# Decoder trunk: each quarter of the second norm transposed once, and the planner taken on through the first two up-projection pairs

## The chip, the cores and the metric

One core of a Trainium2 chip. The metric is the device time of one execution in microseconds (us); lower is better. The engines are TensorE (PE, matmuls and transposes), VectorE (DVE), ScalarE (ACT), GpSimd (POOL) and SyncE (SP, which here issues the transfers). Each runs its own queue in order and waits on semaphores for the others.

## What is computed

One layer of a decoder trunk on x of 1024 x 1024 (tokens x channels), in float32:

```python
h = rmsnorm(x, w_norm_mix)
...                       # h @ w_mix_in, split into three mixers:
...                       # a short gated convolution, a gated DeltaNet of 4 heads (chunked delta rule),
...                       # a stick-breaking attention of 4 heads
x = x + jnp.concatenate([y_sc, y_gdn, y_sb], axis=-1) @ w_mix_out[l]
h = rmsnorm(x, w_norm_ffn[l])
u = causal_dwconv(h @ w_ffn_up[l], w_ffn_conv[l])
gate, val = jnp.split(u, 2, axis=-1)
x = x + (jax.nn.silu(gate) * val) @ w_ffn_down[l]
return rmsnorm(x, w_norm_final)
```

## The kernel before

Tokens come in NB = 8 blocks of 128. Matmuls keep float32 accuracy by splitting each operand into a high and a low part (names ending in h and l) and adding three products, hh, hl and lh.

**The mixing part.** The input projection (`pd`, L314 to L318), the attention (`pz`, `pa`, `po`), and the delta rule, which for each block transposes what `ld` holds (`pv`, `pk`, `pq`), forms `pkq`, solves a triangular system (`py`, `pw`), steps the state (`p1` to `p4`), and ends in `pco` and `pyt`. The decays come as `m` (`m2` with the block's number) from a scratch in memory (`gscr`); the block's result `yg` is written back to `yscr`.

**The output projection.** `mo_mm(n)` computes block n of `pmo` on PE in eight steps (k) of six matmuls of 128x512, DVE adds it to x (`xr`), ACT squares and takes the root, DVE multiplies: h2 of the block, 128 tokens x 1024 channels. Its halves LO and HI, for token blocks 0 to 3 and 4 to 7, are the four quarters B11, B21, B12, B22 of a 2 x 2 partition.

**The up-projection** goes in 22 pairs of 128 gate and 128 value columns (`Pair`, L1524 holds its matmuls). Each pair uses seven products of quarters (m1 to m7, 12 matmuls each) instead of eight. Weights enter as quarters A11, A12, A22 and sums S1 to S4 (`up_sum`), split by `up_split`; activations as seven factors, B11, B21, B22 and the differences T1 to T4, each 4 x 128 x 512 as h and l. The steps e1 to e7 take a product out of PSUM into `ug` and `uv`; ca, cb, cc, cs, cg are the convolution and the gate.

**The factors before.** `mo_tr_p` (and `mo_tr` for block 7) transposes B11 and B21 of blocks 0 to 3. For blocks 4 to 7 POOL forms differences of h2 in token layout, in place; T1 and B22 are transposed (`phT`, `phB`) between steps of `pmo`, and T2, T3 and T4 by `mo_late` between the products of pairs 0 and 1. ACT copies the high part out of PSUM and DVE subtracts it for the low part. That makes 28 groups of four 128x128 transposes.

**What sets the order.** For the mixing part and the output projection a planner, `Flow`, sets the order of every engine: processes (`fl.spawn`) ask for engine time with an estimate and a class (lower first), take and give tokens of each buffer pool, and wait for events (`now`, `wait`). From the first pair on the code's order was written by hand for PE, and the framework ordered DVE, ACT, POOL and SP until pair 1's m7. From pair 2 on all orders are by hand.

## Time and profile before

| | us |
|---|---|
| median of 3 runs | 1229.4 (1226.56 to 1230.95) |
| profiled execution | 1229.95 |
| its span | 1228.2 |
| PE busy | 1194.0 (97%) |
| DVE busy | 942.5 (77%) |
| ACT busy | 634.7 (52%) |
| POOL busy | 404.7 (33%) |

The granted clock of PE was 0.996 of full over the span. The profile's page gives shares over all of the span; the views used further down cut it into stretches, list what PE waited for, and show single instructions with the idle time ahead of them and what ended it. The delta rule's blocks lie between about 342 and 490 us, `pmo1` to `pmo7` between 488 and 576, pairs 0 and 1 between 576 and 637.

### The profile page before, as it was taken

Reading aid. Unit: us, or ns where it says so; the run is one execution under the profiler, and the core shown is the slowest. Engines: PE = TensorE matmul, PEld = TensorE weight load, DVE = VectorE, ACT = ScalarE, POOL = GpSimd, SP = SyncE. Lnnn points to the kernel's source line nnn. Section 1 sums busy time; section 2 is a strip of 40 time slices with the busy share of each in tenths; the row PEclk is TensorE's granted clock in tenths of the full one; section 3 lists DMA queues with packets and bytes.
Section 4 is the critical chain, followed back from the end, with each engine's and each line's share of the span. In section 5 each row is a group of like instructions: output and inputs, shape, how many; then the busy total and the mean of one; then the engine's idle time right before and its main releaser. Section 6 shows DMA issues by size and latency. Waiting matters only on the chain.

```text
span 1228.2 us, 16683 instructions
## 1 busy us (share of the span) xinstructions
PE 1194.0 (97%) x6131; PEld 993.0 (81%) x6131; DVE 942.5 (77%) x1317; ACT 634.7 (52%) x1085; POOL 404.7 (33%) x322
## 2 busy tenths in 40 slices
PE   8999999999999999999899999999999999999997
PEld 6798887887878889777688888888888887888886
DVE  3776789977984769445778888888888878985774
ACT  6766576868334453323554443544545534454554
POOL 3445443434244542014424444345442322001200
PEclk9999999999999999999999999999999999999999
DMA  9111132432352663434122433233332279852314
GB/s 345 56 56 41 56 125 88 123 96 86 111 150 70 154 203 118 155 111 153 35 77 87 129 108 115 74 95 124 112 112 78 95 264 357 300 139 80 103 52 146
DMA packets 87089, 152.76 MB, mean 124 GB/s; under 512 B 6592, under 2 KB 42464, under 8 KB 86752
## 3 DMA queue, kind: packets, MB, share of 16 engines
q1 hardware_dynamic: 86864, 151.59, 38.2%
q8 instruction: 48, 0.79, 0.3%
q14 instruction: 33, 0.27, 0.1%
q10 hardware_dynamic: 144, 0.10, 0.1%
HBM read 110.50 MB, written 41.17 MB: 123 GB/s over the span
## 4 chain that ended last, share of the span: by engine, by line
PE 80%; DVE 6%; ACT 5%; DMA 4%; issue 3%; POOL 1%; SPq 0%; POOLq 0%; ACTq 0%; DVEq 0%
PE pu L1524 18%; PE pz L1524 9%; PE pdx L1693 8%; PE pdzP L1693 7%; PE pd L314 5%; PE pd L316 5%; PE pd L318 5%; PE py L1524 4%; PE pmo L1304 2%; PE pmo L1302 2%; PE pmo L1300 2%; DMA wd<-wdn_in 1%; PE po L687 1%; DMA m<-gscr 1%; PE pa L665 1%
## 5 line engine op out<-in xcount | busy, mean ns | idle before, releaser
L234 POOL TENSOR_TENSOR sg<-sg,om 128x511 f32<-128x511 f32 (+3 forms) x64 | 60.6, 957 | 116.5 <-DVE om L650 60.7
L237 DVE SCALAR_TENSOR_TENSOR ua<-uv,ck,ua 128x1023 f32<-128x1023 f32 (+1 forms) x44 | 76.1, 1730 | 7.3 <-ACT ua L231 7.2
L234 POOL TENSOR_TENSOR ws<-wu 128x512 f32<-128x512 f32 x43 | 66.5, 1567 | 46.1 <-DMA wu<-wup_in 41.8
L237 DVE SCALAR_TENSOR_TENSOR ua<-ug,ck,ua 128x1023 f32<-128x1023 f32 (+1 forms) x44 | 76.1, 1730 | 0.8
L231 ACT ACTIVATE ua<-ug,ck 128x1024 f32<-128x1024 f32 x22 | 25.4, 1154 | 90.5 <-DVE ug L234 90.5
L1618 ACT ACTIVATE ua<-ua 128x1024 f32<-128x1024 f32 x22 | 23.3, 1061 | 80.4 <-DVE ua L237 80.4
L234 POOL TENSOR_TENSOR x<-x,wfb 128x512 f32<-128x512 f32 x8 | 12.8, 1634 | 126.4 <-ACT y L1709 126.4
L234 POOL TENSOR_TENSOR A<-wu,A 128x512 fp32r<-128x512 f32 x13 | 18.0, 1386 | 99.7 <-ACT A L229 99.7
L234 DVE TENSOR_TENSOR S<-ws,S 128x512 fp32r<-128x512 f32 x53 | 40.6, 771 | 9.0 <-ACT S L229 8.0
L234 DVE TENSOR_TENSOR at<-pa,at 128x512 fp32r<-128x512 f32 (+3 forms) x48 | 26.1, 550 | 22.4 <-ACT at L229 22.2
L229 ACT ACTIVATE S<-ws 128x512 fp32r<-128x512 f32 x53 | 33.3, 630 | 16.8 <-DVE ws L234 7.8
L234 POOL TENSOR_TENSOR h<-h,h 128x512 f32<-128x512 f32 x12 | 15.9, 1324 | 78.3 <-DVE h L237 70.6
L1300 PE MATMUL pmo<-wo,yh 128*128 128x512 f32 x128 | 41.4, 404 | 0.0
L229 ACT ACTIVATE at<-pa 128x512 fp32r<-128x512 f32 (+3 forms) x48 | 23.4, 488 | 33.0 <-PE pa L665 31.7
L1302 PE MATMUL pmo<-wo,yh 128*128 128x512 f32 x128 | 39.7, 391 | 0.0
L1304 PE MATMUL pmo<-wo,yr 128*128 128x512 f32 x128 | 39.6, 390 | 0.0
L650 DVE TENSOR_TENSOR_SCAN om<-om 128x512 f32<-128x512 f32 (+3 forms) x32 | 33.7, 1067 | 6.9 <-ACT om L641 6.1
L1524 PE MATMUL pz<-fT1h,S 128*128 128x512 f32 x112 | 37.0, 391 | 1.6 <-DVE S L234 1.1
L234 DVE TENSOR_TENSOR ws<-ws,wu 128x512 f32<-128x512 f32 x22 | 27.0, 1226 | 14.7 <-POOL ws L234 14.7
L1524 PE MATMUL pu<-fT4h,A 128*128 128x512 f32 x104 | 35.4, 402 | 2.1 <-DVE uv L234 2.1
L229 ACT ACTIVATE ug<-pu 128x512 f32<-128x512 f32 x44 | 26.1, 594 | 15.8 <-PE pu L1524 15.7
L1524 PE MATMUL pz<-fB22h,S 128*128 128x512 f32 x104 | 34.1, 389 | 0.0
(1455 smaller groups left out, 4001.5 us busy)
## 6 DMA issues: line engine op xcount, KB each, us to landing
wu<-wup_in SPq DMA_DIRECT2D x44, 512.0 KB, 3.8
gaP<-gst SPq DMA_DIRECT2D x77, 256.0 KB, 3.4
w<-wcm_in SPq DMA_DIRECT2D x23, 512.0 KB, 3.6
wd<-wdn_in SPq DMA_DIRECT2D x44, 256.0 KB, 5.4
gst<-g SPq DMA_DIRECT2D x12, 512.0 KB, 2.7
...
```

The source lines that it names most:

```text
L229: nc.scalar.activation(out_, in_, AF.Copy)
L234: eng.tensor_tensor(out_, a, b, op=op)
L237: nc.vector.scalar_tensor_tensor(out_, a, s, b, op0=op0, op1=op1)
L314: nc.tensor.matmul(ps[th], lhsT=w_h, rhs=xh[k // 2][:, k % 2, th * 512:(th + 1) * 512], start=first, stop=False)
L316: nc.tensor.matmul(ps[th], lhsT=w_h, rhs=xl[k // 2][:, k % 2, th * 512:(th + 1) * 512], start=False, stop=False)
L318: nc.tensor.matmul(ps[th], lhsT=w_l, rhs=xh[k // 2][:, k % 2, th * 512:(th + 1) * 512], start=False, stop=last)
L650: nc.vector.tensor_tensor_scan(om[:, 0:w][:, ::-1], om[:, 0:w][:, ::-1], om[:, 0:w][:, ::-1], init, op0=mul, op1=ALU.bypass)
L1300: nc.tensor.matmul(po[:, c * 512:(c + 1) * 512], lhsT=h, rhs=wh_[:, c * 512:(c + 1) * 512], start=first, stop=False)
L1302: nc.tensor.matmul(po[:, c * 512:(c + 1) * 512], lhsT=h, rhs=wl_[:, c * 512:(c + 1) * 512], start=False, stop=False)
L1304: nc.tensor.matmul(po[:, c * 512:(c + 1) * 512], lhsT=l, rhs=wh_[:, c * 512:(c + 1) * 512], start=False, stop=last)
L1524: nc.tensor.matmul(o, lhsT=w[:, wk], rhs=b[:, k, :], start=first and k + j == 0, stop=k == 3 and j == 2, skip_group_check=not first)
L1693: nc.tensor.matmul(o, lhsT=a[:, tk], rhs=b, start=first and u == 0 and j == 0, stop=u == NU - 1 and j == 2, skip_group_check=not first)
```

## The change

Each quarter of h2 is transposed once. `left_half` does it for B11 and B21 and keeps a raw copy (`raw_b`) beside the split; `right_half` transposes the two quarters of blocks 4 to 7 (`ph12`, `ph22`) in one group of eight, forms t1 and T3 from them, and spawns the rest (`last_two`, `split_f`), so that all differences are made by DVE from transposed quarters. 64 transposes remain of 112. A group waits for the event "mid" of the next block, five steps into it.

The planner runs on to the end of pair 1: `products` asks for PE, `up_op` for the splits, `up_sums` for the sums (DVE, but POOL for pair 2's S1 and S3), `product_out` for e1 to e7, `first_gate` for pair 0's convolution. Pair 0's weights lie in buffers of the pool e8, which has 10 instead of 8, and the planner counts 8 tokens of it instead of 6; the delta rule's processes take tokens of the same pool.

```diff
+        elif r[0] == "sleep":
+            self.at(self.now + r[1], self.resume, proc, cls)
...
-        back, self.now = self.now, t + ns + land + T_AFTER[e]
+        back, self.now = self.now, t + ns + land + (0 if what == "more" else T_AFTER[e])
...
-    BIG = dict(x8=(8, 8192), e8=(8, 8192), at=(2, 4096), cv=(4, 4096), s2=(9, 2048), wr=(2, 4352), wh=(2, 4352), wl=(2, 4352), rb=(1, 4096))
+    BIG = dict(x8=(8, 8192), e8=(10, 8192), at=(2, 4096), cv=(4, 4096), s2=(9, 2048), wr=(2, 4352), wh=(2, 4352), wl=(2, 4352), rb=(1, 4096))
...
-    fl = Flow(mm=2, ms=4, cv=1, s2=9, wr=2, wh=2, wl=2, at=2, e8=6, x8=0)
...
+    fl = Flow(mm=2, ms=4, cv=1, s2=9, wr=2, wh=2, wl=2, at=2, e8=8, x8=0)
...
+        if n >= NB // 2:
+            fl.spawn(right_half(n), 2)
...
-            yield pe(T_STEP, 1000 + n)
+            yield pe(T_STEP, 1000 + n, "more")
...
+            if k == ks[KT // 2]:
+                now("mid", n)
+            if n == NB - 1:
+                fl.give("x8")
...
-        yield take(H2_TAG[n])
-        yield act(D)
-        h2 = cv(f"h2{n}", tag=H2_TAG[n])
+        yield take("at")
+        yield act(D, cls=1)
+        h2 = cv(f"h2{n}", tag="at")
...
+        for half in (LO, HI) if n < NB // 2 else ():
+            fl.spawn(left_half(n, half), 5)
...
+    def turned(ph, src):
         for k in range(4):
             nc.tensor.transpose(out=ph[:, k * P:(k + 1) * P], in_=src[:, k * P:(k + 1) * P], identity=ident)
-        t = slice(n * P, (n + 1) * P)
-        dh, dl = (f[:, :, t] for f in FAC[what])
-        phv = ph.rearrange("p (k t) -> p k t", k=4)
-        copy(dh, phv)
-        tt(nc.vector, dl, phv, f32(dh), sub)
...
-        m = n - NB // 2
-        h1 = mo[m]
-        tt(nc.gpsimd, h1[:, LO], h2[:, LO], h1[:, LO], sub)
-        factor("T1", m, h1[:, LO], e8)
-        factor("B22", m, h2[:, HI], e8)
-        tt(nc.gpsimd, h2[:, LO], h2[:, HI], h2[:, LO], sub)
-        tt(nc.gpsimd, h2[:, HI], h2[:, HI], h1[:, LO], sub)
-        tt(nc.gpsimd, h1[:, HI], h1[:, HI], h2[:, HI], sub)
...
+    def settled(n):
+
+        return wait("mid", n + 1) if n < NB - 1 else ("sleep", 500)
+
+    def left_half(m, half):
+
+        what, tag = ("B11", "wh") if half is LO else ("B21", "wr")
+        if m == 0:
...
+            make_factor(what, e8)
+        if m % 2 == 0:
+            yield take(tag)
+            pair = T([P, 2, HALF], F32, tag, f"r{what}{m}")
+            for a in range(2):
+                raw_b[what, m + a] = pair[:, a, :]
+        yield settled(m)
         yield take("ms")
         yield pe(4 * 109, 500)
...
+        ph = ms(f"ph{what}{m}")
+        turned(ph, mo[m][:, half])
+        now("turned", what, m)
+        dh, dl = tokens(what, m)
         yield act(512)
-        copy(dh, phv)
+        copy(raw_b[what, m], ph)
+        now("raw", what, m)
+        yield act(512)
+        copy(dh, kt(ph))
         yield dve(512, False)
-        tt(nc.vector, dl, phv, f32(dh), sub)
+        tt(nc.vector, dl, kt(ph), f32(dh), sub)
         fl.give("ms")
-
-    def mo_tr_p(n):
+        now("F", what, m)
...
+    def right_half(n):
+        m = n - NT
+        for what in ("B11", "B21"):
+            yield wait("raw", what, m)
+        b11, b21 = raw_b["B11", m], raw_b["B21", m]
+        if m == 0:
+            yield take("e8", 4)
+            for what in ("T1", "B22"):
+                make_factor(what, e8)
+        yield take("s2", 2)
+        now("right", n)
         yield wait("h2", n)
...
+        yield settled(n)
+        yield take("ms", 2)
+        yield pe(8 * 109, 500)
+        p12, p22 = ms(f"ph12{m}"), ms(f"ph22{m}")
+        turned(p12, mo[n][:, LO])
+        turned(p22, mo[n][:, HI])
+        fl.give("at")
+        t1, b22 = s2(f"t1{m}"), s2(f"b22{m}")
+        yield dve(512, False)
+        tt(nc.vector, t1, p12, b11, sub)
+        fl.spawn(split_f("T1", m, t1), 2)
+        yield act(512)
+        copy(b22, p22)
+        yield dve(512, False)
+        tt(nc.vector, b11, b22, p12, sub)
+        fl.spawn(split_f("T3", m, b11), 7)
+        fl.spawn(last_two(m, t1, b22, b21), 2)
+        dh, dl = tokens("B22", m)
+        yield act(512)
+        copy(dh, kt(p22))
+        yield dve(512, False)
+        tt(nc.vector, dl, kt(p22), f32(dh), sub)
+        fl.give("ms", 2)
+        now("F", "B22", m)
+
+    def last_two(m, t1, b22, b21):
+        yield dve(512)
+        tt(nc.vector, b22, b22, t1, sub)
+        fl.spawn(split_f("T2", m, b22), 3)
+        yield dve(512)
+        tt(nc.vector, b21, b21, b22, sub)
+        fl.spawn(split_f("T4", m, b21), 8)
+        yield wait("F", "T1", m)
+        fl.give("s2")
+        yield wait("F", "T2", m)
+        fl.give("s2")
+
+    def split_f(what, m, raw):
+        yield wait("fac", what)
+        dh, dl = tokens(what, m)
+        yield act(512)
+        copy(dh, kt(raw))
+        yield dve(512)
+        tt(nc.vector, dl, kt(raw), f32(dh), sub)
+        now("F", what, m)
+
+    def late_factors():
+        yield wait("loading", 1)
+        for what in ("T2", "T3", "T4"):
+            yield take("x8", 2)
+            make_factor(what, x8)
...
-        if n < NB - 1:
-            fl.spawn(mo_tr_p(n), 5)
+        if n < NT:
+            fl.spawn(give_h2(n), 5)
+    fl.spawn(late_factors(), 5)
+    fl.spawn(give_raw("T3", "wh"), 5)
+    fl.spawn(give_raw("T4", "wr"), 5)
     fl.free["PE"] = FRONT
-    fl.run()
...
-    OP_TAGS = ("s2",) * 4 + ("wh", "wl", "wr") * 2
+    OP_TAGS = ("wl",) * 2 + ("s2",) * 4 + ("wh", "wr") * 2
...
-        if i == 0:
-            raws[i] = [cv(f"wu{i}{a}") for a in range(2)]
-        else:
-            if not up_tiles:
-                up_tiles["raw"] = x8([P, 2, D], "wu")
-                up_tiles["sum"] = x8([P, 4, HALF], "ws")
-            raws[i] = [up_tiles["raw"][:, a, :] for a in range(2)]
+        if i < 2:
+            tile_of = x8 if i else e8
+            up_tiles[i] = tile_of([P, 2, D], f"wu{i}"), tile_of([P, 4, HALF], f"ws{i}")
...
-    up_load(0)
-    up_split(0, "A11")
-    up_split(0, "A12")
-    up_load(1)
-    up_split(1, "A11")
-    up_split(1, "A12")
-    up_sum(0, "S1")
-    up_sum(0, "S2")
-    p0 = Pair(0)
-    p0.place()
-    p0.m1()
-    p0.e1()
-    mo_late("T2")
-    p0.m2()
-    p0.e2()
-    mo_tr(NB - 1)
-    p1 = Pair(1)
-    p1.m1()
-    mo_late("T3")
-    mo_late("T2", NB // 2 - 1)
-    p1.m2()
-    mo_late("T4")
-    mo_late("T3", NB // 2 - 1)
-    mo_late("T4", NB // 2 - 1)
-    p1.place()
-    up_split(0, "S1")
-    up_split(0, "S2")
-    p0.m5()
-    p0.e5()
-    p1.e1()
-    p1.e2()
-    up_sum(0, "S4")
-    up_split(0, "S4")
-    up_sum(0, "S3")
...
-    up_sum(1, "S3")
-    up_split(1, "S1")
-    up_sum(1, "S2")
-    up_split(1, "S2")
-    p0.m3()
-    p0.e3()
-    up_sum(1, "S4")
-    up_split(1, "S4")
-    p0.m7()
-    p0.e7()
-    up_split(1, "A22")
-    up_split(1, "S3")
-    up_load(2)
-    p1.m5()
...
-    up_sum(2, "S1")
-    up_sum(2, "S3")
-    p0.m4()
-    p0.e4()
-    p0.cs()
...
+    OPS = [(0, "A11"), (0, "A12"), (1, "A11"), (1, "A12"), (0, "S1"), (0, "S2"), (0, "S4"), (0, "S3"), (0, "A22"), (1, "S1"),
+           (1, "S2"), (1, "S4"), (1, "A22"), (1, "S3"), (2, "A11"), (2, "S1"), (2, "S2"), (2, "A12"), (2, "S4"), (2, "A22"), (2, "S3")]
+    PRODUCTS = [(0, "m1"), (0, "m2"), (1, "m1"), (1, "m2"), (0, "m5"), (0, "m6"), (0, "m3"), (0, "m7"), (1, "m5"), (0, "m4"),
+                (1, "m6"), (1, "m3"), (1, "m7")]
+    FACTORS = dict(m1=("A11", "B11"), m2=("A12", "B21"), m5=("S1", "T1"), m6=("S2", "T2"), m3=("S4", "B22"), m7=("S3", "T3"),
+                   m4=("A22", "T4"))
+
+    READ = dict(m6="m1", m3="m5", m7="m6", m4="m7")
...
+    def up_weights(i):
+        if i < 2:
+            yield wait(*(("wo", KT - 1) if i else ("post", NB - 1)))
+            yield take(("e8", "x8")[i], 2)
+            now("loading", i)
+        else:
+            for j, what in OPS:
+                if j == i - 1:
+                    yield wait("op", j, what)
+        yield sp(1024)
+        up_load(i)
+        now("wu", i)
...
+    def up_op(k):
+        i, what = OPS[k]
+        tag = OP_TAGS[k % len(OP_TAGS)]
+        if k > 0:
+            yield wait("alloc", k - 1)
+        yield wait(*(("mo_load", NB - 1) if k < 2 else ("right", NB - 1)))
...
+        if what[0] == "S":
+            yield wait("sum", i, what)
+        a11, a12, a21, a22 = quarters(i)
+        src = {"A11": a11, "A12": a12, "A22": a22}.get(what)
+        if src is None:
+            src = up_place(i, what)
+        yield act(512)
+        copy(h, src)
+        yield dve(512)
+        tt(nc.vector, l, src, f32(h), sub)
+        ops[i, what] = h, l
+        now("op", i, what)
...
+    def up_sums(i, which):
+        yield wait("wu", i)
+        for what in which:
+            on_pool = i == 2 and what in ("S1", "S3")
+            yield pool(512) if on_pool else dve(512)
+            up_sum(i, what, nc.gpsimd if on_pool else nc.vector)
+            now("sum", i, what)
...
+    def products():
+        yield wait("mid", NB - 1)
+        for i, m in PRODUCTS:
+            what, fac = FACTORS[m]
+            yield wait("op", i, what)
+            for t in range(NT):
+                yield wait("F", fac, t)
+            if m in READ:
+                yield wait("e", i, READ[m])
+            if m == "m1":
+                yield take("mm")
+                pairs[i] = Pair(i)
+            elif m in ("m2", "m5"):
+                yield take("ms")
+            yield pe(12 * 227, 2000)
+            getattr(pairs[i], m)()
+            tag = OP_TAGS[OPS.index((i, what)) % len(OP_TAGS)]
+            fl.give(tag, 2 if tag == "s2" else 1)
+            if (i, m) != PRODUCTS[-1]:
+                fl.spawn(product_out(i, m), 3)
...
+    def product_out(i, m):
+        if m == "m1":
+            yield wait("xr", NB - 1)
+            yield take(("cv", "at")[i % 2], 2)
+            pairs[i].place()
+            now("place", i)
+        yield wait("place", i)
+        if m in ONTO:
+            yield wait("e", i, ONTO[m])
+        yield act(512) if m in ("m1", "m5", "m6", "m4") else dve(512, False)
+        getattr(pairs[i], "e" + m[1])()
+        if m in ("m2", "m3"):
+            fl.give("ms")
+        now("e", i, m)
...
+    def first_gate():
+        p = pairs
+        taps = 200, 1.05
+        for half, need in ((0, ("m2", "m3")), (1, ("m7", "m4"))):
+            for m in need:
+                yield wait("e", 0, m)
+            yield take("cv")
+            yield act(L)
+            p[0].ca(half)
+            yield dve(L, per=taps)
+            p[0].cb(half)
+            yield dve(L, per=taps)
+            p[0].cc(half)
+            if half == 0:
+                yield act(L, "silu")
+                p[0].cs()
+        yield dve(L)
+        p[0].cg()
...
+    for k in range(len(OPS)):
+        fl.spawn(up_op(k), 4 + k / 4)
+    for i in range(4):
+        fl.spawn(up_weights(i), 5)
+    for i in range(3):
+        fl.spawn(up_sums(i, ("S1", "S2", "S4")), (4.8, 6, 8)[i])
+        fl.spawn(up_sums(i, ("S3",)), (5.2, 6.5, 8)[i])
+    fl.spawn(products(), 5)
+    fl.spawn(first_gate(), 5)
+    fl.run()
+    p1 = pairs[1]
```

**Delta rule, PE.** PE's queue at block 1's `pkq1`, before and then after; `pv2` is block 2's first transpose, `pd21` a part of the input projection.

```order
L318 MATMUL pd21_3150<-xh2_105,w21l_3070 128x512 x2
L1065 MATMUL pkq1_3284<-ld1_3161 128x128 x4
L314 MATMUL pd21_3150<-xh3_107,w21h_3060 128x512 x2
L316 MATMUL pd21_3150<-xl3_108,w21h_3060 128x512 x2
L318 MATMUL pd21_3150<-xh3_107,w21l_3070 128x512 x2
L314 MATMUL pd21_3150<-xh3_107,w21h_3060 128x512 x2
```

```order
L320 MATMUL pd21_3151<-xh2_105,w21l_3071 128x512 x2
L1068 MATMUL pkq1_3293<-ld1_3162 128x128 x4
L1098 MATMUL pv2_3299<-ident_70,ld2_3191 128x128 x4
L316 MATMUL pd21_3151<-xh3_107,w21h_3061 128x512 x2
L318 MATMUL pd21_3151<-xl3_108,w21h_3061 128x512 x2
L320 MATMUL pd21_3151<-xh3_107,w21l_3071 128x512 x2
L1041 MATMUL pk2_3317<-ident_70,ld2_3191 128x128 x4
```

Block 2's `pv2` and `pk2` now stand right behind `pkq1` and after one step of `pd21`; before, two steps of `pd21` followed and block 2's transposes came much later.

**Delta rule, ACT.** ACT's queue where it copies `t644` out of `pw24`, before and after; `m24`, `m25` are decays of blocks 4 and 5 (L1029, in the changed file L1032, takes their exponential).

```order
L229 ACTIVATE w15_4013<-pw5_3955 32x128 x2
L229 ACTIVATE t644_3815<-pw24_4018 64x256
L231 ACTIVATE t645_3848<-py5_4023 32x4x32
L231 ACTIVATE Tt4_3788<-py5_4023 32x4x32 x2
L231 ACTIVATE Tt4_3788<-py24_4040 64x4x64
L1029 ACTIVATE m24_4009<-m24_4009 128x512
```

```order
L1177 ACTIVATE m23_3732<-pco3_4121 128x512
L233 ACTIVATE t644_3956<-py4_4145 32x4x32
L233 ACTIVATE Tt4_3891<-py4_4145 32x4x32 x2
L231 ACTIVATE w15_4170<-pw5_4104 32x128 x2
L1032 ACTIVATE m25_4138<-m25_4138 128x512
L1184 ACTIVATE fo_4165<-fo_4165 128x4
L231 ACTIVATE t644_3956<-pw24_4175 64x256
```

The copy from `pw24` now stands behind the exponential of `m25`; before, it stood ahead of that of `m24`.

**Output projection, PE.** PE's queue in block 5, steps 3 to 5, before and after.

```order
L1304 MATMUL pmo5_5065<-wo3_4142,yr5_4985 128x512 x2
L1388 MATMUL phT10_5108<-ident_70,h20_4741 128x128 x4
L1300 MATMUL pmo5_5065<-wo4_4303,yh51_4987 128x512 x2
L1302 MATMUL pmo5_5065<-wo4_4303,yh51_4987 128x512 x2
L1304 MATMUL pmo5_5065<-wo4_4303,yr5_4985 128x512 x2
L1300 MATMUL pmo5_5065<-wo5_4327,yh51_4987 128x512 x2
L1302 MATMUL pmo5_5065<-wo5_4327,yh51_4987 128x512 x2
L1304 MATMUL pmo5_5065<-wo5_4327,yr5_4985 128x512 x2
L1388 MATMUL phB220_5132<-ident_70,h24_5077 128x128 x4
L1300 MATMUL pmo5_5065<-wo6_4475,yh51_4987 128x512 x2
```

```order
L1314 MATMUL pmo5_5090<-wo3_3900,yr5_5004 128x512 x2
L1310 MATMUL pmo5_5090<-wo4_4055,yh51_5006 128x512 x2
L1312 MATMUL pmo5_5090<-wo4_4055,yh51_5006 128x512 x2
L1314 MATMUL pmo5_5090<-wo4_4055,yr5_5004 128x512 x2
L1365 MATMUL ph120_5137<-ident_70,h24_5102 128x128 x4
L1365 MATMUL ph220_5138<-ident_70,h24_5102 128x128 x4
L1310 MATMUL pmo5_5090<-wo5_4075,yh51_5006 128x512 x2
```

Two groups of four on two half steps have become one group of eight behind step 4.

**First pairs, DVE.** DVE's queue around `uv0`, which is e7 of pair 0, before; and after, first from the sums of pair 1 to the low part of T1 that m5 reads, then around `uv0`.

```order
L234 TENSOR_TENSOR A11_2_5632<-wu_5336,A11_2_5632 128x512
L234 TENSOR_TENSOR ug0_5352<-pz0_5523,ug0_5352 128x512
L234 TENSOR_TENSOR ws_5337<-ws_5337,wu_5336 128x512
L237 SCALAR_TENSOR_TENSOR ua0_5628<-ug0_5352,ck_63,ua0_5628 128x1023
L234 TENSOR_TENSOR uv0_5353<-pu0_5351,uv0_5353 128x512
L237 SCALAR_TENSOR_TENSOR ua0_5628<-ug0_5352,ck_63,ua0_5628 128x1022
```

```order
L236 TENSOR_TENSOR ws1_5296<-wu1_5295 128x512
L236 TENSOR_TENSOR fT3l_5345<-rB110_4717,fT3h_5344 128x4x128 x2
L236 TENSOR_TENSOR fT3l_5345<-rB112_4954,fT3h_5344 128x4x128
L236 TENSOR_TENSOR t13_5450<-ph123_5440,rB112_4954 128x512
L236 TENSOR_TENSOR S2_0l_5453<-ws0_4849,S2_0h_5452 128x512
L236 TENSOR_TENSOR S4_0_5470<-ws0_4849,S4_0_5470 128x512
L236 TENSOR_TENSOR rB112_4954<-b223_5451,ph123_5440 128x512
L236 TENSOR_TENSOR fT1l_5008<-t13_5450,fT1h_5007 128x4x128
```

```order
L236 TENSOR_TENSOR A22_1l_5544<-wu1_5295,A22_1h_5543 128x512
L236 TENSOR_TENSOR S3_1l_5546<-ws1_5296,S3_1h_5545 128x512
L239 SCALAR_TENSOR_TENSOR ua0_5575<-ug0_5398,ck_63,ua0_5575 128x1023
L236 TENSOR_TENSOR uv0_5399<-pu0_5321,uv0_5399 128x512
L239 SCALAR_TENSOR_TENSOR ua0_5575<-ug0_5398,ck_63,ua0_5575 128x1022
```

Before, the sum `ws` of pair 2, which needs POOL's, stood two places ahead of `uv0`; now the splits of pair 1 do. `fT1l` has three low parts of T3, t13, a split, S4 and a difference ahead of it.

## Rows read from the trace of the kernel before

**Rows 1.** Table of stretches: window, length, busy us (count) per engine, granted clock, DMA.
```profile
342.00:464.00 122.00, 116.20 (x1028) 98.84 (x1027) 81.96 (x158) 56.74 (x138) 54.65 (x73) 0.99 0.49 137
...
576.00:600.00 24.00, 21.42 (x119) 17.15 (x118) 18.05 (x26) 13.12 (x25) 12.02 (x10) 1.00 0.06 23
600.00:625.00 25.00, 22.86 (x94) 18.50 (x93) 19.07 (x22) 14.27 (x21) 8.15 (x7) 0.93 0.28 85
...
700.00:998.00 298.00, 298.00 (x1316) 246.74 (x1316) 259.82 (x248) 138.95 (x216) 122.25 (x78) 1.00 0.33 104
```

**Rows 2.** Waits of PE, 485 to 640 us: total us, times, longest.
```profile
PE pu L1524 <- DVE uv L234: 2.1, 1, 2.1
PE phT L1388 <- POOL h L234: 1.3, 3, 0.6
...
PE phB L1388 <- DVE h L237: 0.8, 3, 0.3
```

**Rows 3.** Timeline of PE in block 1 (start, us, ..., [idle before <-releaser]).
```profile
504.88 0.62 PE L1302 MATMUL pmo<-wo,yh 128*128 128x512 f32 x2
505.33 0.61 PE L1304 MATMUL pmo<-wo,yr 128*128 128x512 f32 x2
506.21 0.66 PE L1388 MATMUL phB<-ident,h 128*128 128x128 f32 x4 [0.27 <-DVE h L237]
506.62 0.70 PE L1300 MATMUL pmo<-wo,yh 128*128 128x512 f32 x2
```

**Rows 4.** Timeline of PE, two groups of eight transposes.
```profile
463.03 1.04 PE L1095 MATMUL pv<-ident,ld 128*128 128x128 f32 x8
463.90 1.04 PE L1038 MATMUL pk<-ident,ld 128*128 128x128 f32 x8
```

**Rows 5.** Timeline of PE, first matmul of p0.m4 and the one after its last.
```profile
613.14 0.79 PE L1524 MATMUL pu<-fT4h,A 128*128 128x512 f32 x1 [2.14 <-DVE uv L234]
...
617.54 0.39 PE L1524 MATMUL pu<-fT2h,S_1h 128*128 128x512 f32 x1
```

**Rows 6.** Timeline of PE in the delta-rule blocks.
```profile
351.24 1.16 PE L1065 MATMUL pkq<-ld 128*128 128x128 f32 x8 [1.20 <-DVE m L237]
352.15 0.71 PE L314 MATMUL pd<-xh,w21h 128*128 128x512 f32 x2
...
397.77 0.63 PE L1193 MATMUL pyt<-ident,on 128*128 128x128 f32 x4 [0.59 <-DVE on L234]
...
406.97 1.16 PE L1142 MATMUL p<-vn,m 128*128 128x128 f32 x8 [2.12 <-ACT vn L229]
...
408.37 1.20 PE L314 MATMUL pd<-xh,w25h 128*128 128x512 f32 x2
...
411.07 0.63 PE L1165 MATMUL pco<-S,ld 128*128 128x128 f32 x2
```

**Rows 7.** Timeline of ACT, the release of pq0's buffer.
```profile
353.79 0.58 ACT L1076 ACTIVATE m<-pq 128x512 f32<-128x512 f32 x1
```

**Rows 8.** DMA issues, 340 to 490 us: count, KB each, median us to landing.
```profile
m<-gscr SPq DMA_DIRECT2D x7, 256.0 KB, 5.3
```

**Rows 9.** Timeline of ACT, a table load.
```profile
492.08 1.28 ACT L1319 ACT_TABLE_LOAD   x1
493.37 0.29 ACT L1319 ACTIVATE q<-q,eps 128x1 f32<-128x1 f32 x1
```

**Rows 10.** Timelines of DVE and of POOL in blocks 1 and 4.
```profile
506.52 0.69 DVE L234 TENSOR_TENSOR yr<-yr,yh 128x512 fp32r<-128x512 f32 x1 [0.37 <-ACT yh L229]
...
538.86 1.22 DVE L234 TENSOR_TENSOR xr<-xr,pmo 128x1024 f32<-128x1024 f32 x1 [2.79 <-PE pmo L1304]
...
541.83 1.28 DVE L237 SCALAR_TENSOR_TENSOR h<-xr,q,wnb 128x1024 f32<-128x1024 f32 x1
543.30 1.82 DVE L234 TENSOR_TENSOR yr<-yr,yh 128x512 fp32r<-128x512 f32 x1 [0.19 <-ACT yh L229]
...
543.28 1.29 POOL L234 TENSOR_TENSOR h<-h,h 128x512 f32<-128x512 f32 x1 [62.00 <-DVE h L237]
```

More of the change, by code (lines that the diff above doesn't have):

```diff
@@ L1335, in trunk, with kt, tokens @@
     HALF = D // 2
+    LO, HI = slice(0, HALF), slice(HALF, D)
     FAC = {}
-    H2_TAG = ("wr", "wr", "wh", "wh", "wl", "wl", "at", "at")
-    def factor(what, n, src, tile_of):
-        if what not in FAC:
-            FAC[what] = [tile_of([P, 4, HALF], f"f{what}{a}", F32R) for a in "hl"]
-        ph = ms(f"ph{what}{n}")
+    NT = NB // 2
+    raw_b = {}
+    def kt(ap):
+        return ap.rearrange("p (k t) -> p k t", k=4)
+    def tokens(what, m):
+        return [f[:, :, m * P:(m + 1) * P] for f in FAC[what]]
@@ L1369, in mo_late @@
-    def mo_late(what, last=None):
-        for m in range(NB // 2 - 1) if last is None else (last,):
-            h1, h2 = mo[m], mo[m + NB // 2]
-            factor(what, m, {"T2": h2[:, HI], "T3": h2[:, LO], "T4": h1[:, HI]}[what], x8)
-    begun = set()
-    def factor_p(what, n, src):
-        if what not in begun:
-            begun.add(what)
-            yield take("e8", 2)
-            now("fac", what)
-        yield wait("fac", what)
+    def settled(n):
+        return wait("mid", n + 1) if n < NB - 1 else ("sleep", 500)
@@ L1418, in trunk, with give_raw @@
+    def late_factors():
[3 more added lines that the diff above has]
+            make_factor(what, x8)
+    def give_raw(what, tag):
+        for m in range(NT):
+            yield wait("F", what, m)
+            if m % 2:
+                fl.give(tag)
     for c in range(2):
@@ L1497, in up_sum @@
         if what == "S1":
-            tt(nc.gpsimd, o, a21, a22, add)
+            tt(eng or nc.gpsimd, o, a21, a22, add)
         elif what == "S2":
@@ new lines, in up_op @@
+    def up_op(k):
[4 more added lines that the diff above has]
+        yield wait(*(("mo_load", NB - 1) if k < 2 else ("right", NB - 1)))
+        yield take(tag, 2 if tag == "s2" else 1)
+        h, l = op_tile(f"{what}_{i}")
+        now("alloc", k)
+        yield wait("wu", i)
[11 more added lines that the diff above has]
+        now("op", i, what)
```

102 lines of the change are left out of this document (22 added, 80 removed).

## The prediction, made before the changed kernel ran

> **What bounds the kernel now.** I read the table of stretches first. From 700 to 998 us, the long run of up-projection pairs, TensorE (PE) is busy for all of the time [rows 1], and the change leaves every engine's order from pair 3 on as it was; nothing can be won or lost there. In the two stretches at the start of the up-projection PE stands idle for 2.58 of 24 and 2.14 of 25 us, while VectorE (DVE) is busy for 75% and 76% of them, and in the delta rule's stretch PE is idle for 5.8 of 122 [rows 1]: PE sets the end, and what counts is its instructions and the moments when it stands still. The table of waits names those moments: three waits for POOL's differences of h2 quarters, three for h2 itself, and one of 2.1 us for DVE's `uv` [rows 2]. The timeline then gives what each costs, which is more than the idle time printed, since consecutive matmuls otherwise overlap. A step of two matmuls goes on 0.455 us after the one before; the transposes of block 1 start 0.88 us after it [rows 3], so a printed wait of 0.27 costs 0.42. I add 0.16 to each wait for that.
>
> All sums are against the profiled execution, 1229.95 us (span 1228.2), 0.55 above the median of 1229.4.
>
> **Part 1: 48 transposes fewer.** A lone group of four takes 0.41 us to the next start [rows 3], and the first matmuls behind it start some 0.07 to 0.1 late: 0.48. Eight in a row take 0.87, or 0.109 each [rows 4]. Before, 14 lone groups stand in or around the blocks and the other 56 transposes come in longer rows: 14 x 0.48 + 56 x 0.109 = 12.8. Afterwards there are eight groups of eight, each 0.87 plus at most 0.1: 7.0 to 7.8. Gain 5.0 to 5.8; I take **-5.4**. All of it lies on PE, which is the path here.
>
> **Part 2: waits in the output projection and the first two pairs.** In blocks 1 to 7 the transposes now come after five of eight steps, 6.8 us after the previous block's end, and h2 is ready 4.3 us after it (add, square, root, product on two engines); the differences no longer stand ahead of them. The six waits of [rows 2] in the blocks, 2.1 us printed and 3.0 with the overlap, go. What is late next is DVE: a second-half block gives it the add of 1.22, h2 at 1.28, up to two yr differences and eight operations on quarters at 0.69 [rows 10], 9.4 us of a block's 11.8, some 10 with the up-projection's first splits; it just keeps up. In the pairs, PE loses 4.7 us idle [rows 1], in seven waits, 5.8 with the overlap; the largest is the 2.14 ahead of p0.m4, where `uv` stood behind a sum that waited for POOL. And m4's twelve matmuls took 4.40 us [rows 5] instead of the 2.72 of a product at full clock: the granted clock, 0.93 over 600 to 625 us [rows 1], was at its lower level, 1.2 GHz, right behind that wait: 1.7 more. Together 3.0 + 5.8 + 1.7 = 10.5. In the changed order p0's e7 stands behind DVE work that needs no POOL, and p1.m5 lies between m7 and m4, which hides it. New there: T1's last low part. DVE has three fT3l, then t13, S2_0l, S4_0 and rB112 ahead of fT1l; five operations at 0.69 [rows 10] from 0.4 us after the end of block 7's transposes (9.0 us after pmo7) make it ready near 12.9 us, and PE, with four products and eight transposes, stands at p0.m5 at 11.7. That is 1.2 us (0 if the three fT3l are done early, 3 if DVE carries a backlog out of block 7), 0.3 more ahead of m6, and I keep 1.0 for small ones: 2.5. Part 2 is 2.5 - 10.5 = **-8.0**, bounds -5 and -10.
>
> **Part 3: the delta-rule blocks, moved by two more tokens of the e8 pool.** Here the change takes and gives. Of its 5.8 us of idle time there [rows 1], 1.5 lie before 352 us; the rest are five waits, the first of 2.12 [rows 6], 4.2 together and 5.0 with the overlap, and behind the 2.12 six pd matmuls took 2.70 us from start to start instead of about 1.4 [rows 6], and the matmuls on either side are longer too, 1.6 together: 6.6. All five waits go or shrink, since block 2's loads, with m22 among them, are issued before its turn. New: pv2 stands right behind pkq1 in PE's queue. It needs the PSUM buffer that ACT frees by m<-pq, which ends at 354.37 [rows 7], and PE is free at 352.15 [rows 6]: 2.2 us, with four groups of pd work queued behind it that before filled this time. Next, pk5 needs the buffer that ACT frees by t644, now queued behind the exponential of m25, whose load SP issues behind the write of yg2. Write, load of 5.3 us [rows 8] and exponential bring it 7.5 to 8.5 us after pyt2, where PE arrives after 6.1: 1.4 to 2.4, say 1.9. p42 behind m24's exponential the same way 1.0, py20 0.4, small ones 0.5. Last, pyt7: the square root of block 0's norm now lies among the delta rule's logarithms and exponentials on ACT, which makes 42 table loads of 37. One takes 1.28, and the next instruction starts at once [rows 9]; the chain to pyt7 holds two or three of them and comes 1.15 late. Sum 7.15. The clock fell to 1.2 GHz after idle spells of 2.12 and 2.14 us [rows 5, 6] and not after the 1.20 at 351 us [rows 6]; I price one fall at 1.6 behind pv2 (about 2.0 printed) and 0.6 as a share of one behind pk5. 7.15 + 2.2 = 9.4, less 6.6: **+2.8**, bounds -2 (pk5 and pyt7 covered, no fall) and +6 (both falls, late loads).
>
> A rule speaks against the table loads. The trace first: the load at 492.08 takes 1.28 us, the next activation starts at 493.37, and neither row has idle time before it [rows 9]. The Trainium skill, page "ScalarE: Activation LUTs", section "What ACT_TABLE_LOAD costs", adds a drain of about 1.38 us to every switch. By that pyt7 would be late by 2.8 to 4.1 more and the sum 1222 to 1223; this trace shows no such drain, so the row decides.
>
> The sum: -5.4 - 8.0 + 2.8 = -10.6; 1229.95 - 10.6 = 1219.4 profiled, 1218.8 as a median. **Forecast 1219 us**, own range 1215.5 to 1222.5.
>
> POOL's 16 subtractions go and cost nothing before but the waits counted; the loads of pair 0 are issued earlier and hidden, and the one load moved forward on SP (wd2) collides with nothing PE waits for.
>
> **Rivals.**
> *The delta rule does not suffer.* Its old waits go, pv2 alone stays at 2.2 without a fall of the clock, pk5 and pyt7 come in time because PE gets there later than I count. Then part 3 is 2.2 + 1.0 - 6.6 = -3.4 and the time 1229.4 - 5.4 - 8.0 - 3.4 = about **1212 to 1213**. For it: all waits there are under 2.2 us and their sizes are counted by hand. Against: pv2's follows from two rows alone.
>
> *The waits only change place.* Part 3 at its upper bound, +6, and DVE late at p0.m5 by 3 with a fall of the clock behind it (1.7), so part 2 is -5: 1229.4 - 5.4 - 5 + 6 = **1225**, between 1223 and 1228. For it: DVE has under 2 us of slack in a second-half block, and a new order's waits are easily missed. Against: p0.m5 is hardly ever further behind than the few operations named.
>
> *DVE becomes the bound, slower than before.* The change lays 24 operations with both sources in SBUF on DVE: 16 low parts of T1 to T4, which read PSUM before, and eight differences, which were POOL's. Such an operation takes 0.69 us with POOL idle and took 1.8 at 543.30, with POOL at a subtraction from 543.28 [rows 10]. At 0.6 more for each of the 24, half of that excess, DVE has 14.4 us more to do in blocks 4 to 7 and pair 0, no slack is left to hide it, and the time is 1219 + 14.4 = **1233**; it decides against the change from 18 of the 24 on (10.6 / 0.6). Against it: POOL's own 16 subtractions leave this very stretch, and only four sums remain there. The Trainium skill, page "SBUF — State Buffer", says in its text on the shared port pair that a VectorE operation with two SBUF inputs and a GpSimd operation that reads SBUF shut each other out. The two times of [rows 10] agree with it; by it the operations are slow only while POOL works, which here is nearly never.
>
> **Chances.** Forecast 0.58; delta rule does not suffer 0.14; waits change place 0.20 (0.08 of it still faster by over 0.3%); DVE the bound 0.08. With 0.3% (3.7 us, about what a measurement of this kernel tells from no change) the borders are 1225.7 and 1233.1. Faster 0.58 + 0.14 + 0.08 = 0.80, same 0.12, slower 0.08. The range takes in the first case, most of the second and the nearer half of the third: 1211 to 1226.
>
> **What would show it.** In the blocks no PE wait for h or POOL, and eight groups of transposes of 0.87 us. A PE wait of about 2 us ahead of pv2 near 352, with the clock lower behind it, and one of 1 to 2.4 ahead of pk5. A wait of about 1.2 for fT1l ahead of p0.m5, none ahead of m4, and no half clock there. It is wrong if the blocks and the first two pairs together are not shorter by 10 to 15 us, if the delta-rule stretch grows by over 6 us or shrinks by over 2, or if the operations on quarters run near 1.2 us on DVE.

## The result and the profile after

The changed kernel takes 1222.2 us (median of 7 runs, 1218.69 to 1226.06) against 1229.4 (7 runs): ratio 0.9944, 95% interval 0.9927 to 0.9961, some 7 us less. The forecast was 1219. The profiled execution took 1226.06 us, with a span of 1224.3; it is the longest of the seven; its clock is a part of the reason, as the last section shows. First its page: span, PE's busy time, and the granted clock in 40 slices.

```profile
span 1224.3 us, 16593 instructions
PE 1191.8 (97%) x6083; PEld 992.8 (81%) x6083; DVE 939.8 (77%) x1340; ACT 646.7 (53%) x1102; POOL 373.3 (30%) x299
...
PEclk9999999999998989999999999999999999999999
```

Slices 13 and 15 (367 to 398 and 428 to 459 us) stand below 9; before, all stood at 9. Next the table of stretches (window, length, then busy us and count for PE, PE's weight loads, DVE, ACT and POOL, then granted clock, DMA share, GB/s), which answers to [rows 1].

```profile
350.00:360.00 10.00, 7.20 (x32) 5.63 (x32) 8.98 (x21) 3.09 (x7) 1.60 (x3) 0.83 0.75 198
...
520.00:583.00 63.00, 63.00 (x301) 52.49 (x300) 38.31 (x55) 26.97 (x53) 0.00 (x0) 1.00 0.44 139
583.00:600.00 17.00, 16.24 (x75) 12.89 (x74) 16.59 (x28) 10.68 (x21) 0.00 (x0) 1.00 0.17 63
600.00:632.00 32.00, 32.00 (x143) 26.49 (x142) 26.04 (x33) 17.60 (x27) 6.13 (x4) 1.00 0.18 58
```

From 520 to 632 us, the blocks of the output projection and the first two pairs, PE stands idle for 0.76 us in all. From 350 to 360, in the delta rule, it stands for 2.8 of 10, at a granted clock of 0.83. The waits of PE say the same: first 342 to 470 us, then 470 to 640 (total us, times, longest), which answers to [rows 2].

```profile
PE pk L1041 <- ACT t L231: 2.8, 1, 2.8
PE pv L1098 <- ACT m L1079: 2.0, 1, 2.0
...
PE pyt L1196 <- DVE on L236: 1.2, 1, 1.2
PE pz L1571 <- DVE fT1l L236: 0.8, 1, 0.8
```

No block waits for h or POOL any more and p0.m4 does not wait for `uv`. New are the wait ahead of `pv` in the delta rule and most of the one ahead of `pk` (0.49 us before).

From the starts of four instructions in each trace, the time splits as follows.

| us, one profiled execution each | before | after | difference |
|---|---|---|---|
| from block 1's `pkq` to the first matmul of `pmo2` (delta rule, blocks 0 and 1 of the output projection) | 150.46 | 160.24 | +9.8 |
| from there to p0.m1 (blocks 2 to 7) | 74.38 | 70.84 | -3.5 |
| from p0.m1 to pair 2's m2 (first two pairs) | 60.49 | 48.50 | -12.0 |
| from there to the end of PE's last matmul | 584.28 | 585.15 | +0.9 |

So in these two executions the later blocks and the first two pairs are 15.5 us shorter, and the delta rule's stretch is 9.8 longer; in a second profile of the changed kernel (`after_again` below) that stretch takes 159.47, 9.0 longer. The stretch ahead of block 1's `pkq` adds 1.0, of which the last section tells the cause. The 0.9 at the end belongs to the change without the tokens (585.23 in `hold_e8` below, 584.29 in `before_e8`); I did not follow it further.

### The profile page after: what moved, and what is told of

It reads as the page before. It is cut to its first block, busy times and chain, and to the rows that moved or that the text cites. A ratio compares the mean times of both kernels' runs of the same rounds, so it can differ in the third digit from the quotient of the medians.

```text
span 1224.3 us, 16593 instructions
## 1 busy us (share of the span) xinstructions
PE 1191.8 (97%) x6083; PEld 992.8 (81%) x6083; DVE 939.8 (77%) x1340; ACT 646.7 (53%) x1102; POOL 373.3 (30%) x299
## 4 chain that ended last, share of the span: by engine, by line
PE 81%; DVE 5%; DMA 5%; ACT 4%; issue 2%; SPq 1%; POOL 1%; ACTq 0%; DVEq 0%; POOLq 0%
PE pu L1571 19%; PE pz L1571 10%; PE pdx L1739 8%; PE pdzP L1739 7%; PE pd L316 6%; PE pd L318 5%; PE pd L320 5%; PE py L1571 4%; PE pmo L1310 2%; PE pmo L1312 2%; PE pmo L1314 2%; DMA m<-gscr 1%; PE po L690 1%; DMA xs<-x_in 1%; PE pa L668 1%
## 5 line engine op out<-in xcount | busy, mean ns | idle before, releaser
L236 POOL TENSOR_TENSOR ws<-wu 128x512 f32<-128x512 f32 x40 | 62.1, 1573 | 172.4 <-DMA wu<-wup_in 172.4
L236 DVE TENSOR_TENSOR A<-wu,A 128x512 fp32r<-128x512 f32 x29 | 28.4, 983 | 11.7 <-ACT A L231 11.7
L1571 PE MATMUL py<-fB21h,A 128*128 128x512 f32 x112 | 36.7, 389 | 0.0
L1571 PE MATMUL pz<-fB22h,S 128*128 128x512 f32 x112 | 36.7, 389 | 0.0
L1571 PE MATMUL pu<-fB11h,A 128*128 128x512 f32 x104 | 34.1, 389 | 0.0
L1571 PE MATMUL pu<-fT3h,S 128*128 128x512 f32 x104 | 34.1, 389 | 0.0
```

The costliest lines, as they stand in the source:

```text
L236: eng.tensor_tensor(out_, a, b, op=op)
L1571: nc.tensor.matmul(o, lhsT=w[:, wk], rhs=b[:, k, :], start=first and k + j == 0, stop=k == 3 and j == 2, skip_group_check=not first)
```

## The experiments

Each is timed against the kernel before on the same chip; the first four form one group, the next four (`before_e7`, `pv2_swap`, `pool_diff`, `hold_land`) a second, the last three a third. Across groups I compare ratios.

**The two halves of the change apart.** The pool e8 and its two tokens set when the delta rule's preparation starts; all else of the change lies behind it. `hold_e8` keeps all of the change but gives those two tokens late; `before_e8` is the kernel before with them alone. `after_again` is the changed kernel once more.

```diff
 # hold_e8, from the changed kernel
-    fl = Flow(... e8=8, x8=0)
+    fl = Flow(... e8=6, x8=0)
...
+    def held():
+        yield wait("m2", NB - 1)
+        fl.give("e8", 2)
+    fl.spawn(held(), 5)
 # before_e8, from the kernel before
-    BIG = dict(x8=(8, 8192), e8=(8, 8192), ...
+    BIG = dict(x8=(8, 8192), e8=(10, 8192), ...
-    fl = Flow(... e8=6, x8=0)
+    fl = Flow(... e8=8, x8=0)
```

> The changed kernel again, as the measure for the other three. 1222 us, ratio to before 0.994. If the idle spells ahead of pv2 (2.0 us) and pk5 (2.8 us) cause the falls of the clock, the clock is at 1.2 GHz again right behind both in a new profile; if the falls are chance, they lie elsewhere. The fall at 62 us, where the program is as before, should not come back in every execution.

> The changed kernel, but the planner holds the two more e8 tokens back until block 7 of the delta rule has its buffers, so that all engines' orders there are those of the kernel before up to the output projection's first block; all else of the change stays. Theory (the tokens move the delta rule's preparation and this gives some 9 us back): 1213 us, ratio 0.987, no wait ahead of pv2 or pk5, the old 2.1 us wait of p4 back. Rival (the loss there has another cause: classes of the norm, or the first block's mixing with the delta rule): 1220 to 1224.

> The kernel before with this one part of the change: e8 with 10 buffers and 8 tokens. The delta rule's orders become those of the changed kernel up to the first block of the output projection; the transposes and the hand-written first pairs stay. Theory: slower by what the delta rule loses, about 8 us: 1237, ratio 1.0065, with waits of about 2.0 ahead of pv2 and 2.8 ahead of pk5. Rival: within 2 us of 1229.

Measured: `after_again` 1221.8 us, ratio 0.9944 (0.9928 to 0.9960). `hold_e8` 1216.0, ratio 0.9895 (0.9882 to 0.9908). `before_e8` 1237.5, ratio 1.0067 (1.0046 to 1.0089). The waits of PE between 342 and 640 us in `hold_e8`, then in `before_e8`:

```profile
PE p L1145 <- ACT vn L231: 1.9, 1, 1.9
...
PE pk L1041 <- ACT t L231: 0.8, 1, 0.8
```

```profile
PE pv L1095 <- ACT m L1076: 2.0, 1, 2.0
PE pk L1038 <- ACT t L229: 1.9, 1, 1.9
```

The wait ahead of pv and most of that ahead of pk come with the tokens and go with them. The tokens cost 8.4 us on the kernel before (1237.45 - 1229.09) and 5.7 on the changed one (1221.77 - 1216.04); by the intervals the two do not differ. `before_e8` took the time that was expected, with a smaller wait ahead of pk (1.9, not 2.8); `hold_e8` did not quite: some 9 us back were expected, 1213. All else of the change gains 13.0 us (1229.09 - 1216.04). So the change is two changes, one worth 13 us and one that gives 6 to 8 of it back, and `hold_e8` beats both kernels. `hold_e8` ran again in the third group:

> hold_e8 again, as the measure for the next two and to see whether its gain holds on another chip: ratio to before 0.9895, about 1216, with a wait of some 2 us ahead of p4.

Measured: 1216.0, ratio 0.9884 (0.9871 to 0.9897). The gain holds.

**What a transpose costs.** `twice` issues each of the 64 transposes twice; no order changes.

```diff
     def turned(ph, src):
-        for k in range(4):
+        for k in (0, 1, 2, 3, 0, 1, 2, 3):
```

> The changed kernel with each of its 64 transposes issued twice into the same buffer; all orders stay. By part 1 of the prediction (0.109 us for each transpose, all on PE's path): 7.0 us more than the changed kernel, 1229. Rival (PE has slack behind the groups, so that fewer transposes gain little): under 3 us more, 1225 or less.

Measured: 1229.7, ratio 1.0002 (0.9989 to 1.0014), 8 us above `after_again`; the ratios differ by 0.0058, 7.1 us, give or take 2.5. A group in the changed kernel, and the same in `twice` (timeline of PE: start, us, the instruction):

```profile
554.74 1.04 PE L1365 MATMUL ph<-ident,h 128*128 128x128 f32 x8
555.53 0.70 PE L1310 MATMUL pmo<-wo,yh 128*128 128x512 f32 x2
```

```profile
567.80 1.91 PE L1365 MATMUL ph<-ident,h 128*128 128x128 f32 x16
569.47 0.71 PE L1310 MATMUL pmo<-wo,yh 128*128 128x512 f32 x2
```

0.79 us against 1.67 to the next start: 0.11 for each transpose, as in [rows 4]. From the first matmul of `pmo2` to p0.m1, with six of the eight groups, it is 75.92 us against 70.84: 0.85 for each doubled group, so there the transposes lie on PE's path. In the first pairs the one doubled group costs nothing: from p0.m1 to pair 2's m2 it is 48.52 us against 48.50, because p0.m5's wait of 0.8 for `fT1l` vanishes. There a transpose lies beside DVE's work.

**The wait for `uv` alone.** `before_e7` is the kernel before with DVE's order taken by hand from p0.m7 to the end of pair 1, which puts `uv` ahead of pair 2's sum.

```diff
+    first = ExitStack()
+    first.enter_context(tc.manual_schedule(engines={E.DVE}))
     p0.m7()
     p0.e7()
...
     p1.m7()
+    first.close()
     ordered = ExitStack()
```

> The kernel before with DVE's order from p0.m7 to pair 1's end by hand: e7 of pair 0 (uv) comes ahead of pair 2's sum, which waits for POOL; nothing else of the change. By part 2 of the prediction this one wait cost 2.14 + 0.16 and 1.7 for the clock: 4.0 us less than the kernel before, 1225, no wait ahead of p0.m4 and no fall of the clock near 613 us. Rival (the wait only moves to a later product): under 1 us less.

Measured: 1227.5, ratio 0.9982 (0.9971 to 0.9993), 2.5 us instead of the 4.0 expected. The wait for `uv` is gone, but the clock fell earlier, behind a smaller wait that both kernels have:

```profile
600.68 0.78 PE L1524 MATMUL pz<-fT1h,S 128*128 128x512 f32 x2 [1.09 <-DVE S L234]
601.26 0.63 PE L1524 MATMUL pz<-fT1l,S 128*128 128x512 f32 x1
601.68 1.05 PE L1524 MATMUL pz<-fT1h,S 128*128 128x512 f32 x2
```

Matmuls of 128x512 go on 0.43 us apart there instead of 0.23 (1.2 GHz). In the kernel before, the same wait, 1.08 us, was followed by full speed. From p0.m1 to pair 2's m2 the profile has 58.20 us against 60.49, with one spell at the lower clock in both: so the idle part of this term, 2.3, is shown. The clock part, 1.7, is not: in this execution, the longest of the twelve, the fall went to another place, and over all runs the mean granted clock is 0.9959 against 0.9951, which is 1 us at most.

**One wait in the delta rule.** `pv2_swap` is the changed kernel with one step of `pd21` ahead of pv2 on PE instead of behind it.

```diff
         pv = ms(f"pv{n}")
+        def turn():
             for h in range(GH):
                 nc.tensor.transpose(out=pv[:, h * P:(h + 1) * P], ...
+        if n == 2:
+            behind.append(turn)      # called after the next step of dense()
+        else:
+            turn()
```

> The changed kernel with one swap on PE: one step of pd21 (six matmuls, 1.37 us) ahead of pv2 instead of behind it; all else in the same order. Theory (the wait ahead of pv2 and the fall of the clock behind it both count): the wait falls from 2.0 to 0.6 us, the clock stays up behind it, 1.4 + 1.6 = 3 us less than the changed kernel: 1219. Rival (the delta rule's chain of DVE, ACT and transfers sets this stretch, so what PE saves here it waits for at the next place): the waits ahead of pk5 and the others grow by as much, 1221.5 to 1222.

Measured: 1221.0, ratio 0.9926 (0.9909 to 0.9943). PE around pv2, and the stretch (columns as above):

```profile
354.79 0.61 PE L320 MATMUL pd<-xh,w21l 128*128 128x512 f32 x2
356.05 0.66 PE L1104 MATMUL pv<-ident,ld 128*128 128x128 f32 x4 [0.65 <-ACT m L1083]
357.45 0.66 PE L1045 MATMUL pk<-ident,ld 128*128 128x128 f32 x4 [0.75 <-DVE ld L236]
```

```profile
352.00:364.00 12.00, 9.74 (x51) 7.88 (x52) 12.00 (x25) 4.28 (x9) 5.34 (x6) 1.00 0.38 102
```

The wait is 0.65 and the clock stays at full speed behind it (1.00, where the changed kernel had 0.83). The ratio is 0.0018 below that of `after_again`, 2.2 us, but the two intervals overlap, and the time, 1221.0, lies between the theory's 1219 and the rival's 1221.5. The rival, that PE waits at the next place for what it saves here, is half of what the profile shows: of the 1.4 us saved, 0.75 comes back at once ahead of pk2. PE's waits between 342 us and pyt7 are 9.1 us in sum, as in the changed kernel (9.1, and 8.9 in `after_again`). What went is the fall of the clock behind pv2; how much the swap gains stays open.

**Whether DVE is hindered by POOL.** `pool_diff` is `hold_e8` with eight differences back on POOL.

```diff
-        yield dve(512)
-        tt(nc.vector, b22, b22, t1, sub)
+        yield pool(512)
+        tt(nc.gpsimd, b22, b22, t1, sub)
...
-        tt(nc.vector, b21, b21, b22, sub)
+        tt(nc.gpsimd, b21, b21, b22, sub)
```

> hold_e8 with the eight differences that make T2 and T4 back on POOL (128x512, 1.3 us each) instead of DVE. Rival of the prediction (DVE operations with both sources in SBUF are slow beside POOL): DVE's low parts that meet one of them take 1.2 to 1.8 us instead of 0.69, T2's low parts come late and m6 waits, 2 to 5 us more than hold_e8's 1216. If they do not hinder each other: within 1 us of 1216, operations on quarters at 0.69.

Measured: 1220.4, ratio 0.9920 (0.9901 to 0.9938), some 3 to 4 us above `hold_e8`. The timelines of POOL, of DVE, of ACT and of PE (one row at p0.m7) around block 7 and behind it:

```profile
562.47 1.28 POOL L236 TENSOR_TENSOR rB<-rB,b 128x512 f32<-128x512 f32 x1
...
589.29 4.13 POOL L236 TENSOR_TENSOR rB<-rB,b 128x512 f32<-128x512 f32 x1
...
589.18 0.68 DVE L236 TENSOR_TENSOR fT3l<-rB,fT3h 128x512 fp32r<-128x512 f32 x1
590.38 0.68 DVE L236 TENSOR_TENSOR fT2l<-b,fT2h 128x512 fp32r<-128x512 f32 x1
...
593.45 0.63 ACT L231 ACTIVATE fT4h<-rB 128x512 fp32r<-128x512 f32 x1 [1.89 <-POOL rB L236]
...
597.22 0.50 PE L1576 MATMUL pu<-fT3h,S 128*128 128x512 f32 x1 [0.56 <-ACT ug L231]
```

The loss is there, but not by the path that was expected: it is POOL that pays. A subtraction that took 1.28 at other places takes 4.13 us beside a row of DVE operations with two SBUF inputs, and those keep 0.68. Pair 0's m6 shows no wait. ACT's queue stands 1.89 us for the late difference and copies `ug` behind it, and PE waits 0.56 ahead of p0.m7. Another 0.70 ahead of p1.m7 is for `ug` too; its cause I did not follow. From p0.m1 to pair 2's m2 the profile has 50.66 us against 48.51 in `hold_e8`; from there to PE's last matmul it is another 1.3 longer, which I did not follow either. The rule of the Trainium skill (page "SBUF — State Buffer", section "SBUF: two separate sides") is that the two shut each other out. The run agrees, and it shows that POOL, which starts at 589.29 behind DVE at 589.18, is shut out at length when DVE has one such operation behind another. In [rows 10] DVE had started 0.02 us behind POOL and was the loser.

**Other plans of the delta rule.** If early preparation is harmful only through pv2 and pk5, a better plan of the same kind should win. Three were tried: one token held back instead of two (`hold_e8_7`), pv2's process told to start later (`pv2_late`), and `hold_e8` with the planner told that loads take 5.5 us (`hold_land`).

```diff
 # hold_e8_7: as hold_e8, with e8=7 and fl.give("e8", 1)
 # pv2_late, from the changed kernel, in prep_v
+        if n == 2:
+            yield "sleep", 2500
         yield take("ms")
 # hold_land, from hold_e8, in prep3, for both kinds of load
-        yield sp(256)
+        yield "SP", 5500, None, None
```

> The changed kernel with one of the two e8 tokens held back until block 7 of the delta rule has its buffers: block 3's loads go early, block 2's decays m22 do not, and pv2 stands where it stood before; the orders first differ from hold_e8's some 115 rows later on PE. Theory (what costs is pv2 and pk2 put right behind pkq1, and pk5 behind m25's load): if both need the second token, as hold_e8, 1215 to 1217. Rival (any earlier loading of ld3 crowds the transfers and ACT): between hold_e8 and the changed kernel, 1218 to 1220.

> The changed kernel with both tokens, but the planner told to start block 2's first transpose 2.5 us later, and planning anew from there. Theory (the early preparation is harmful only where it stands right behind pkq1; m22 loaded early is a gain of the old 2.1 us wait and its clock): no wait ahead of pv2, none of 2 us ahead of p4, at or under hold_e8, 1214 to 1217. Rival (the whole earlier plan runs ahead of its transfers): the wait ahead of pk5 or others stays at 2 us and more, 1219 to 1222.

> hold_e8 with the planner told that the delta rule's loads land 5.5 us after their issue (it counts 3.3; the trace of the kernel before has 5.3 to 6.1). Theory (PE's waits there come from orders planned on too early loads): the 1.9 us wait of p4 and its fall of the clock go, 2 to 4 us less than hold_e8: 1212 to 1214. Rival (the waits come from other work, so a new plan only moves them): 1215 to 1218.

Measured: 1221.8 (0.9930, 0.9918 to 0.9942), 1220.5 (0.9916, 0.9900 to 0.9932) and 1219.8 (0.9914, 0.9894 to 0.9934). By the medians all are slower than `hold_e8`, and `hold_e8_7` by more than the intervals; that of `hold_land` overlaps with both of `hold_e8`. `hold_e8_7` and `hold_land` lie above the forecasts of the theory and of its rival, `pv2_late` where the rival put it. The longest wait of PE in each, in that order:

```profile
PE py L962 <- DVE ld L236: 4.6, 1, 4.6
```

```profile
PE py L985 <- ACT t L231: 2.5, 1, 2.5
```

```profile
PE pw L949 <- DVE m L236: 4.8, 1, 4.8
```

Each new plan removes the wait it was made for and has a new one of 2.5 to 4.8 us elsewhere. So the theory that only pv2 and pk5 are at fault falls. PE's waits between 342 us and pyt7 are 7.1 to 10.9 us in sum in every plan of this stretch that differs from that of the kernel before, and 5.3 to 6.1 with that plan (`before`, `hold_e8`, `hold_e8_b`). Why these plans all miss (which of the planner's estimates is off) stays open; a longer time for the loads alone did not mend it.

## Why the prediction was right, and where a term was off

The result lies 0.3 us inside the range, and the number alone does not say that the sum was right: parts 1 and 2 were right together, part 3 was not. One of the signs of being wrong came up, a delta-rule stretch that grows by over 6 us: it grew by 9.8 and 9.0 in the two profiles of the changed kernel and by 6.9 in that of `before_e8`.

**Part 1, the transposes (-5.4).** Right as far as shown: 0.109 us each by [rows 4], 0.11 by `twice`, and six of the eight groups are shown to lie on PE's path. What the 14 lone groups cost beyond that, 0.48 each, no run takes apart from the waits.

**Part 2, the waits in the blocks and pairs (-8.0).** Right. With part 1 it makes -13.4; `hold_e8`, which is the change without the tokens, gained 13.0. The wait for T1's last low part was forecast at 1.2 us with DVE's queue as the reason, and it is 0.8, in that queue (timeline of DVE: start, us, instruction):

```profile
591.36 1.89 DVE L236 TENSOR_TENSOR fT3l<-rB,fT3h 128x512 fp32r<-128x512 f32 x3
593.17 0.68 DVE L236 TENSOR_TENSOR t<-ph,rB 128x512 f32<-128x512 f32 x1
...
595.57 0.68 DVE L236 TENSOR_TENSOR fT1l<-t,fT1h 128x512 fp32r<-128x512 f32 x1
```

Three `fT3l`, then t13 at 593.17, and `fT1l` only at 595.57: the order is the one counted, and the operations stand 0.60 apart where 0.69 was taken. The wait for `uv` went, but `before_e7` shows that its clock part (1.7) is not tied to that wait alone. All three profiles with the pairs of the kernel before have one spell at the lower clock in them, at 613.1, 605.0 (`before_e8`) and 601.2 us (`before_e7`); none of the ten profiles with the changed pairs has one there. So that part was gained, with all the pairs' waits and not with one.

**Part 3, the delta rule (+2.8, bounds -2 and +6).** The mechanism was right, the size was not: 8.4 us on the kernel before, 5.7 on the changed one, so at the upper bound or above it. The two largest waits are the ones that were named, with the causes that were named. PE, and for each wait the ACT instructions that end it:

```profile
354.81 0.58 ACT L1079 ACTIVATE m<-pq 128x512 f32<-128x512 f32 x1
355.44 0.87 PE L1098 MATMUL pv<-ident,ld 128*128 128x128 f32 x4 [2.01 <-ACT m L1079]
355.97 1.20 PE L316 MATMUL pd<-xh,w21h 128*128 128x512 f32 x2
...
448.17 0.63 ACT L1032 ACTIVATE m<-m 128x512 f32<-128x512 f32 x1 [3.61 <-DMA m<-gscr]
448.92 0.38 ACT L231 ACTIVATE t<-pw 64x256 f32<-64x256 f32 x1
449.35 1.11 PE L1041 MATMUL pk<-ident,ld 128*128 128x128 f32 x4 [2.85 <-ACT t L231]
```

2.01 us ahead of pv2, where some 2.0 was forecast, and the next pd matmuls are long, 1.0 us for two. pk5, where 1.9 was forecast, waited 2.85 here, 2.36 in `after_again` and 1.89 in `before_e8`. pyt7 waited 1.2 (1.15 forecast) behind two table loads on ACT, of which this is the second:

```profile
506.91 1.28 ACT L1186 ACT_TABLE_LOAD   x1
508.20 0.20 ACT L1186 ACTIVATE fo<-fo 128x4 f32<-128x4 f32 x1
```

The drain that the Trainium skill, page "ScalarE: Activation LUTs", section "What ACT_TABLE_LOAD costs", adds to a load would by an estimate from its figure, 1.38 us for each of the two, have made this wait 2.8 longer; the next activation starts at once, and the trace shows no drain.

The term that failed most is the clock: one fall of 1.6 and a share of 0.6 were counted as new, 2.2 in all, against 1.6 of the kernel before that would go. The trace has three spells at 1.2 GHz in this stretch (windows cut at them; the 0.50 is the granted clock):

```profile
355.75:359.16 3.41, 3.41 (x13) 2.73 (x12) 3.41 (x9) 0.36 (x2) 0.19 (x1) 0.50 0.23 63
...
389.88:396.70 6.82, 6.82 (x29) 5.90 (x29) 0.00 (x0) 1.09 (x3) 3.91 (x4) 0.50 0.25 77
...
447.91:454.73 6.82, 5.38 (x26) 4.37 (x27) 3.98 (x11) 2.84 (x9) 1.08 (x2) 0.50 0.36 98
```

Together 17 us at half speed, where the kernel before had 3.4. At full load half of such a spell is lost, so they cost up to 8.5 in this execution, less where PE stood still anyway. But executions differ. Of the four profiles with these orders in the delta rule, `after` and `after_again` have 17 us at half speed there, `before_e8` has 10.2, and `twice` only the spell behind pv2, 3.4 (columns as above):

```profile
352.00:364.00 12.00, 8.30 (x39) 6.55 (x38) 10.48 (x22) 4.54 (x9) 1.92 (x4) 0.86 0.52 141
364.00:420.00 56.00, 54.49 (x454) 45.25 (x453) 30.26 (x47) 24.23 (x58) 33.78 (x36) 1.00 0.32 93
```

The granted clock of all runs is the better measure. Its mean is 0.9951 for the kernel before and 0.9922 for `before_e8`, 0.9960 for `hold_e8` and 0.9937 for `after_again`. Of spans of 1214 to 1233 us these differences are, as an estimate, 3.6 and 2.8 us lost to the clock by the tokens, where 0.6 net had been counted. That leaves 4.8 and 2.9 of the 8.4 and 5.7 us for the waits, where 2.2 had been counted (7.15 less 5.0). So the clock is the larger part of what part 3 under-priced on the changed kernel, and about half of it on the kernel before.

**The rivals.** That the delta rule does not suffer is excluded by `before_e8`. That DVE becomes the bound is excluded too: its quarter operations ran at 0.68 in the changed kernel, and even with POOL put back beside them. That waits only change place held in the delta rule and nowhere else; the result lies midway between it (1225) and the forecast, so it is the split by stretches and runs that tells them apart, and not the time.
